# Where 16 of 256 gathered rows stand: beside the last tile's gate weights or beside the second table's first chunks

## The chip, the cores and the metric

The kernel runs on one core of one Trainium2 chip. The time is device microseconds of one execution. Timed runs are compared as medians; the profile is of one further execution, whose own time is given with it.

## The reference, cut to what matters

The program is one layer of a latent-token generator: 512 latent tokens and 256 context tokens of width 1024 go through an adaLN, two token mixers (retention and a gated linear recurrence), a merge and a residual. Then comes the part in which the change lies, a product-key expert layer. Each of the 512 tokens picks, for each of 8 heads, 16 of 16,384 single-neuron experts, so 128 experts per token, with softmax weights `g`:

```
act = gelu(einsum('thkd,td->thk', u_tab[e], xb))
out = einsum('thk,thkd->td', g * act, v_tab[e])
```

`u_tab` and `v_tab` are the first and the second table, 16,384 rows of 1024 floats each. A last residual and RMSNorm give the output.

## The kernel before, in words

The 512 tokens are four tiles of 128. Three of them (`DT = 384` tokens, `ndt = 3`) are computed densely. For each of 128 chunks of 128 experts, an S stage (`s_stage`, line 747) multiplies the chunk of the first table with the 384 tokens: load `w` (line 86), split it on ACT and DVE into high and low halves `wh` and `wl`, 24 matmuls into `pS`, and `gelu` by ACT into `gt` (line 753). At most 14 `gt` tiles are held (`RING`); the first 52 chunks (`SPILL`) are written to DRAM (`gd`) and come back later as `gr`. `pS` has two PSUM buffers, `w` two buffers, `wh` and `wl` four.

The gate weights say which expert each token uses, and with what weight. For each dense tile and each of 8 groups of 16 tokens, DVE builds one-hot tiles (lines 884 to 887: `ohB`, `ohAl`, `ohAh`, `ohAl`), TensorE multiplies them (`pw`, lines 893 and 894, 32 matmuls per group), ACT copies the products into `stg` (line 895), and SP stores `stg` to `wd` in DRAM (line 898). 24 groups make up the whole `wd`.

The second table follows in a loop of 128 chunks (line 956): load `vw`, split it into `vwh` and `vwl`, multiply `gt` or `gr` by the gate weights `wt` into `af` (line 975, DVE), split that into `ah` and `al`, and add 18 matmuls per chunk into `po`. `wt` is read back from `wd` by SP, eight chunks at a time (line 950). Each such load takes a slice of all 24 groups, so the first one waits for the last store. The S stages that are left run among these chunks.

The fourth tile (number 3, third in `TORD`) is computed by gathering. `gather_rows` (line 795) is a generator of 128 steps on the first table and 128 on the second. One step issues an indirect DMA from POOL, 128 rows of 4 KB, into one of four `row` buffers, and one DVE instruction on it (line 800, later 811). A "gathered row" below is one such step. The table of numbers in line 43, the count in line 902 and that in line 995 say how many steps have been issued by each group of the last dense tile (tile 2) and by each chunk of the second table.

The order of the instructions on each engine is fixed when the program is built: a scheduler places them by its own timeline of the program. Each engine then takes its instructions in that order, and SP and POOL issue their DMAs in that order. So a change in the number of steps can move other instructions too.

Of the kernel before, what the change touches and what calls it, by code (L numbers as in the profile page):

```python
# [39 lines left out]
NCOLS = _n  # L40
DT = 384
SPILL, RING = 52, 14
GFIRST, GSTEPS, SSTEPS = 10, 252, 124
AHEAD = 2
NROW = 4
TORD = (0, 1, 3, 2)
# [6 lines left out]
def block_kernel(ctx: ExitStack, tc: tile.TileContext, A):  # L53
# [6 lines left out]
    def split(hi, lo, src):  # L60
        S.activation(hi, src, AF.Copy)  # L61
        V.tensor_tensor(lo, src, f(hi), op=OP.subtract)  # L62

    def mm3(out, wh, wl, xh, xl, start, stop):
        PE.matmul(out, wh, xh, start=start, stop=False)  # L65
        PE.matmul(out, wh, xl, start=False, stop=False)  # L66
        PE.matmul(out, wl, xh, start=False, stop=stop)  # L67
# [693 lines left out]
    def s_more(n=1):  # L761
        nonlocal s_next
        for _ in range(n):
            if s_next < 128:
                s_stage(s_next)
                s_next += 1
# [28 lines left out]
    def gather_rows():  # L795
        for j in range(128):
            row = gp.tile([128, D], F32, name="row", bufs=4)
            G.indirect_dma_start(out=row, out_offset=None, in_=A["u"],  # L798
                                 in_offset=bass.IndirectOffsetOnAxis(ap=ei[:, j:j + 1], axis=0))
            V.scalar_tensor_tensor(row, row, 1.0, h2t, op0=OP.mult, op1=OP.mult, accum_out=act[:, j:j + 1])  # L800
            yield
        S.activation(act, act, AF.Gelu_apprx_tanh)
        V.tensor_tensor(act, act, gg, op=OP.mult)
        for j in range(128):
            row = gp.tile([128, D], F32, name="row", bufs=4)
            G.indirect_dma_start(out=row, out_offset=None, in_=A["v"],  # L806
                                 in_offset=bass.IndirectOffsetOnAxis(ap=ei[:, j:j + 1], axis=0))
            if j == 0:
                V.tensor_scalar(acc, row, act[:, j:j + 1], None, op0=OP.mult)
            else:  # L810
                V.scalar_tensor_tensor(acc, row, act[:, j:j + 1], acc, op0=OP.mult, op1=OP.add)  # L811
            yield

    with ExitStack() as es:
# [37 lines left out]
        gen = None  # L852
        for t in TORD:
            if t == ndt:
                gather_prep(p1)
                gen = gather_rows()
# [55 lines left out]
    def finish(t, src, xt):  # L912
        xo = gp.tile([128, D], F32, name="xo", tag="row", bufs=4)
        ss = gp.tile([128, 2], F32, name="ss", bufs=4)
        hs = [slice(512 * n, 512 * n + 512) for n in range(2)]
        for n, o in enumerate(hs):
            V.tensor_tensor(xo[:, o], src[:, o], g2r[:, o], op=OP.mult)
            V.tensor_tensor(xo[:, o], xo[:, o], xt[:, o], op=OP.add)
            S.activation(xt[:, o], xo[:, o], AF.Square, accum_out=ss[:, n:n + 1])
        V.tensor_tensor(ss[:, 0:1], ss[:, 0:1], ss[:, 1:2], op=OP.add)  # L920
        S.activation(ss[:, 0:1], ss[:, 0:1], AF.Sqrt, scale=1.0 / D, bias=epsc)
        V.reciprocal(ss[:, 0:1], ss[:, 0:1])
        for o in hs:
            V.scalar_tensor_tensor(xo[:, o], xo[:, o], ss[:, 0:1], fgr[:, o], op0=OP.mult, op1=OP.mult)
            SY.dma_start(A["out"][0, 128 * t:128 * t + 128, o], xo[:, o])

    def load_x1(t):
        if t in (1, 2):
            xt = ph.tile([128, D], F32, name="xt", tag="vw", bufs=2)
        else:  # L930
            xt = gp.tile([128, D], F32, name="xt", tag="row", bufs=4)
        SY.dma_start(xt, x1d[:, t])
        return xt
# [12 lines left out]
    def table(j):  # L946
        gr = j // WI
        if gr not in wts:
            wt = ph.tile([128, NG_, WI, WG], F32, name="wt" if WI * gr + WI > SPILL else "wu", bufs=2)
            SY.dma_start(wt, wd[:, :, WI * gr:WI * gr + WI, :])  # L950
            wts[gr] = wt
        return wts[gr]
# [3 lines left out]
    for n_, j in enumerate(order):  # L956
        ring = j >= SPILL
        while s_next < min(128, s_first + (128 - s_first) * (n_ + 1) // SSTEPS) or (ring and s_next <= j):
            s_more()
        if ring:  # L960
            a = Gs.pop(j)
        else:
            a = ph.tile([128, DT], F32, name="gr", bufs=2)
            SY.dma_start(a, gd[:, j])
        wt = table(j)
        v = ph.tile([128, D], F32, name="vw", bufs=2)
        vd = SY.dma_start(v, A["v"][128 * j:128 * j + 128])

        with tc.issue_after(vd.ins):
            table(order[min(n_ + 3, 127)])  # L970
        vh, vl = (ph.tile([128, D], F32R, name=f"vw{m}", bufs=2) for m in "hl")
        ah, al = (ph.tile([128, DT], F32R, name=f"a{m}", bufs=2) for m in "hl")
        split(vh, vl, v)
        af = ph.tile([128, DT], F32, name="af")
        paced = V.tensor_tensor(af.rearrange("p (g t) -> p g t", t=WG), a.rearrange("p (g t) -> p g t", t=WG), wt[:, :, j % WI], op=OP.mult)
        split(ah, al, af)
        last.append((ah, al, vh, vl))
        if n_ == 125:

            g2r, fgr = (wst.tile([128, KT, 128], F32, name=nm, tag="w").rearrange("p n m -> p (n m)") for nm in ("g2r", "fgr"))  # L980
            SY.dma_start(g2r, g2d.to_broadcast([128, D]))
            SY.dma_start(fgr, A["fg"].to_broadcast([128, D]))
            with tc.issue_after(paced.ins):
                S.activation(gp.tile([128, 1], F32, name="ws"), epsc, AF.Sqrt)
        if n_ != 126:
            for t in range(ndt):
                for n in range(2):
                    for i, (ah, al, vh, vl) in enumerate(last):
                        mm3(outs[t][:, 512 * n:512 * n + 512], ah[:, 128 * t:128 * t + 128], al[:, 128 * t:128 * t + 128],
                            vh[:, 512 * n:512 * n + 512], vl[:, 512 * n:512 * n + 512], n_ == 0, n_ == 127 and i == 1)  # L990
                if n_ == 127:
                    finish(t, outs[t], load_x1(t))
            last = []
        with tc.issue_after(paced.ins):
            while gen and done < GFIRST + GSTEPS * (n_ + 1) // 128:
                done += 1
                if next(gen, 1):
                    gen = None
                    finish(ndt, acc, load_x1(ndt))
# [64 lines left out]
```

## Time and profile before

| | us |
|---|---|
| median of 3 timed runs | 1871.71 (1871.47 to 1877.47) |
| the profiled execution's own time | 1868.65 |
| its span | 1866.9 |
| PE busy | 1812.8 (97%) |
| DVE busy | 1511.8 (81%) |
| ACT busy | 822.2 (44%) |
| POOL busy | 377.7 (20%) |

PE is TensorE, PEld its weight loads, DVE VectorE, ACT ScalarE, POOL GpSimd; SP issues most DMAs. Matmuls overlap each other, so the busy time of PE is not the time of its matmuls added up; what is told from it below is when it sat idle. Times in the trace count from the start of the span. The gate weights of tile 2 lie at about 969 to 1043 us, the second table's loop from about 1060 us to the end.

### The profile page before, as it was taken

How to read it: one execution, taken by the hardware profiler on the slowest of the kernel's cores; microseconds unless marked ns; L12 is line 12 of the kernel's file. 1: busy time of each engine (PE TensorE's matmuls, PEld its weight loads, DVE VectorE, ACT ScalarE, POOL GpSimd, SP SyncE). 2: the span in 40 equal slices, each digit the busy share in tenths (PEclk: the TensorE clock that was granted, in tenths of full speed). 3: DMA queues.
4: the chain of work that ended last, by engine and by line, in shares of the span. 5: the costliest groups of instructions: out<-in, count | busy, mean ns of one | idle time of the engine just before them, and what ended most of it. 6: DMA issues, size and time to landing. Idle time of an engine off the chain costs nothing.

```text
span 1866.9 us, 26880 instructions
## 1 busy us (share of the span) xinstructions
PE 1812.8 (97%) x9953; PEld 1598.3 (86%) x9953; DVE 1511.8 (81%) x2793; ACT 822.2 (44%) x1203; POOL 377.7 (20%) x327
## 2 busy tenths in 40 slices
PE   7899999999999999999999989999999999999997
PEld 3788888887878989999999978888888888888886
DVE  8988777788853679999988678877787878788788
ACT  4666575765222444445545433333333333333323
POOL 0000000000000000000031244444454444344440
PEclk9999999999999999999999999999999999999999
DMA  7122121215953433657778989999999899998985
GB/s 312 52 68 69 57 69 57 69 57 175 327 157 102 153 107 105 189 188 246 253 283 281 320 323 348 337 330 320 345 339 344 316 340 339 355 329 320 347 308 206
DMA packets 173320, 431.27 MB, mean 231 GB/s; under 512 B 14850, under 2 KB 84610, under 8 KB 168708
## 3 DMA queue, kind: packets, MB, share of 16 engines
q1 hardware_dynamic: 136324, 295.31, 47.0%
q0 software_dynamic: 36864, 134.23, 19.7%
q8 instruction: 78, 1.28, 0.3%
q14 instruction: 54, 0.44, 0.1%
HBM read 388.86 MB, written 40.64 MB: 230 GB/s over the span
## 4 chain that ended last, share of the span: by engine, by line
PE 75%; DVE 11%; DMA 9%; ACT 2%; issue 2%; SPq 0%; DVEq 0%; POOL 0%; ACTq 0%; POOLq 0%
PE po L65 9%; PE po L66 9%; PE po L67 9%; PE pS L65 8%; PE pS L66 8%; PE pS L67 8%; DMA vw<-in_v_dram 5%; DMA modb<-in_mod_t_dram 2%; DVE wl L62 2%; PE pw L893 1%; PE pw L894 1%; PE pu L66 1%; PE pu L67 1%; PE pu L65 1%; PE p L66 1%
## 5 line engine op out<-in xcount | busy, mean ns | idle before, releaser
L61 ACT ACTIVATE wh<-w 128x1024 fp32r<-128x1024 f32 (+1 forms) x216 | 224.9, 1043 | 340.8 <-PE pS L66 76.9
L65 PE MATMUL pS<-h2h,wh 128*128 128x384 f32 x1024 | 346.5, 338 | 2.4 <-ACT gt L753 2.2
L67 PE MATMUL pS<-h2h,wl 128*128 128x384 f32 x1024 | 345.5, 337 | 0.7 <-DVE wl L62 0.7
L66 PE MATMUL pS<-h2l,wh 128*128 128x384 f32 x1024 | 345.5, 337 | 0.0
L62 DVE TENSOR_TENSOR wl<-w,wh 128x1024 fp32r<-128x1024 f32 (+1 forms) x216 | 258.9, 1200 | 84.3 <-ACT wh L61 81.9
L798 POOL DMA_INDIRECT row<-in_u_dram,ei x128 | 190.3, 1487 | 564.3 <-DVE row L800 288.3
L66 PE MATMUL po<-vwl,ah 128*128 128x512 f32 x768 | 300.2, 391 | 0.0
L67 PE MATMUL po<-vwh,al 128*128 128x512 f32 x768 | 299.8, 391 | 0.0
L65 PE MATMUL po<-vwh,ah 128*128 128x512 f32 x768 | 267.0, 395 | 10.1 <-ACT vwh L61 10.1
L61 ACT ACTIVATE ah<-af 128x384 fp32r<-128x384 f32 x128 | 67.1, 524 | 382.1 <-PE po L66 261.1
L806 POOL DMA_INDIRECT row<-in_v_dram,ei x128 | 177.6, 1387 | 224.4 <-DVE acc L811 193.1
L65 PEld LDWEIGHTS pS<-h2h,wh 128*128 128x128 f32 x1024 | 192.6, 188 | 9.6 <-ACT gt L753 3.3
L62 DVE TENSOR_TENSOR vwl<-vw,vwh 128x1024 fp32r<-128x1024 f32 x128 | 156.3, 1221 | 53.3 <-ACT vwh L61 53.1
L67 PEld LDWEIGHTS pS<-h2h,wl 128*128 128x128 f32 x1024 | 192.5, 188 | 6.2 <-DVE wl L62 1.0
L66 PEld LDWEIGHTS pS<-h2l,wh 128*128 128x128 f32 x1024 | 192.6, 188 | 5.4
L65 PEld LDWEIGHTS po<-vwh,ah 128*128 128x128 f32 x768 | 143.0, 188 | 37.0 <-ACT vwh L61 11.7
L61 ACT ACTIVATE vwh<-vw 128x1024 fp32r<-128x1024 f32 x128 | 134.6, 1051 | 84.7 <-DMA vw<-in_v_dram 79.3
L66 PEld LDWEIGHTS po<-vwl,ah 128*128 128x128 f32 x768 | 144.3, 188 | 27.6 <-DVE vwl L62 0.4
L67 PEld LDWEIGHTS po<-vwh,al 128*128 128x128 f32 x768 | 144.4, 188 | 27.3
L811 DVE SCALAR_TENSOR_TENSOR acc<-row,act,acc 128x1024 f32<-128x1024 f32 x127 | 162.5, 1280 | 4.4 <-DMA row<-in_v_dram,ei 4.2
L800 DVE SCALAR_TENSOR_TENSOR row<-row,h2t 128x1024 f32<-128x1024 f32 x128 | 153.4, 1219 | 1.7 <-DMA row<-in_u_dram,ei 1.5
L62 DVE TENSOR_TENSOR al<-af,ah 128x384 fp32r<-128x384 f32 x128 | 71.1, 556 | 79.2 <-ACT ah L61 78.9
(368 smaller groups left out, 3489.5 us busy)
## 6 DMA issues: line engine op xcount, KB each, us to landing
w<-in_uT_dram SPq DMA_DIRECT2D x128, 512.0 KB, 4.8
vw<-in_v_dram SPq DMA_DIRECT2D x128, 512.0 KB, 6.6
w<-in_w_in_dram SPq DMA_DIRECT2D x48, 512.0 KB, 3.6
wd<-stg SPq DMA_DIRECT2D x24, 1024.0 KB, 6.0
modb<-in_mod_t_dram SPq DMA_DIRECT2D x32, 512.0 KB, 5.2
wt<-wd SPq DMA_DIRECT2D x10, 1536.0 KB, 15.9
gd<-gt SPq DMA_DIRECT2D x52, 192.0 KB, 3.3
gr<-gd SPq DMA_DIRECT2D x52, 192.0 KB, 6.7
```

Source lines behind the costliest of these rows:

```text
L61: S.activation(hi, src, AF.Copy)
L62: V.tensor_tensor(lo, src, f(hi), op=OP.subtract)
L65: PE.matmul(out, wh, xh, start=start, stop=False)
L66: PE.matmul(out, wh, xl, start=False, stop=False)
L67: PE.matmul(out, wl, xh, start=False, stop=stop)
L798: G.indirect_dma_start(out=row, out_offset=None, in_=A["u"], in_offset=bass.IndirectOffsetOnAxis(ap=ei[:, j:j + 1], axis=0))
L800: V.scalar_tensor_tensor(row, row, 1.0, h2t, op0=OP.mult, op1=OP.mult, accum_out=act[:, j:j + 1])
L806: G.indirect_dma_start(out=row, out_offset=None, in_=A["v"], in_offset=bass.IndirectOffsetOnAxis(ap=ei[:, j:j + 1], axis=0))
L811: V.scalar_tensor_tensor(acc, row, act[:, j:j + 1], acc, op0=OP.mult, op1=OP.add)
L893: PE.matmul(pw[:, i], B[:, xg, :, xi], Ah[:, xg, :, xi], start=True, stop=False)
L894: PE.matmul(pw[:, i], B[:, xg, :, xi], Al[:, xg, :, xi], start=False, stop=True)
```

## The change

Two numbers of line 43 and the expression of line 995 change:

```
-GFIRST, GSTEPS, SSTEPS = 10, 252, 124
+GFIRST, GSTEPS, SSTEPS = 26, 236, 124
...
-            while gen and done < GFIRST + GSTEPS * (n_ + 1) // 128:
+            while gen and done < GFIRST + GSTEPS * max(0, n_ - 3) // 124:
```

Before, 10 rows are issued beside the 8 groups of tile 2, and chunk `n_` brings the count to 10 + 252 (n_ + 1) // 128: 11, 13, 15 and 17 after the first four chunks, then about 1.97 more per chunk. After, 26 rows are issued beside the 8 groups (by group: 3, 6, 9, 13, 16, 19, 22, 26), none in the chunks 0 to 3, then about 1.90 per chunk. In both the generator ends in chunk 125. The S stages' own pace (`s_more`) is not edited.

On DVE, at the fifth and sixth group of tile 2, before (`row`, line 800, is a gathered row; `wl` an S stage's low half):

```order
L884 TENSOR_TENSOR ohB<-iota,e2T 128x2048
L885 TENSOR_TENSOR ohAl<-iota,e1T 128x2048
L800 SCALAR_TENSOR_TENSOR row,act<-row,h2t 128x1024
L62 TENSOR_TENSOR wl<-w,wh 128x1024
L886 TENSOR_TENSOR ohAh<-ohAl,ghT 128x2048
L884 TENSOR_TENSOR ohB<-iota,e2T 128x2048
L885 TENSOR_TENSOR ohAl<-iota,e1T 128x2048
L800 SCALAR_TENSOR_TENSOR row,act<-row,h2t 128x1024
L887 TENSOR_TENSOR ohAl<-ohAl,glT 128x2048
L62 TENSOR_TENSOR wl<-w,wh 128x1024
L886 TENSOR_TENSOR ohAh<-ohAl,ghT 128x2048
```

and the same engine at the same groups after:

```order
L884 TENSOR_TENSOR ohB<-iota,e2T 128x2048
L885 TENSOR_TENSOR ohAl<-iota,e1T 128x2048
L800 SCALAR_TENSOR_TENSOR row,act<-row,h2t 128x1024 x2
L887 TENSOR_TENSOR ohAl<-ohAl,glT 128x2048
L800 SCALAR_TENSOR_TENSOR row,act<-row,h2t 128x1024
L886 TENSOR_TENSOR ohAh<-ohAl,ghT 128x2048
L800 SCALAR_TENSOR_TENSOR row,act<-row,h2t 128x1024
L62 TENSOR_TENSOR wl<-w,wh 128x1024 x2
L887 TENSOR_TENSOR ohAl<-ohAl,glT 128x2048
L884 TENSOR_TENSOR ohB<-iota,e2T 128x2048
L885 TENSOR_TENSOR ohAl<-iota,e1T 128x2048
L800 SCALAR_TENSOR_TENSOR row,act<-row,h2t 128x1024 x3
```

The rows stand three or four to a group in place of one or two, between the one-hot instructions of a group.

On ACT, at the end of the gate weights and the start of the second table, before (`gt` is the last step of an S stage, `stg` of a gate-weight group, `ah` belongs to the first chunk of the second table):

```order
L895 ACTIVATE stg_10540<-pw_10568 128x128x4
L61 ACTIVATE wh_10850<-w_10848 128x1024
L895 ACTIVATE stg_10540<-pw_10578 128x128x4
L61 ACTIVATE wh_10957<-w_10955 128x1024
L753 ACTIVATE gt_10652<-pS_10621 128x384
L61 ACTIVATE wh_11064<-w_11062 128x1024
L753 ACTIVATE gt_10685<-pS_10654 128x384
L61 ACTIVATE wh_11169<-w_11167 128x1024
L753 ACTIVATE gt_10771<-pS_10740 128x384
L61 ACTIVATE ah_10711<-af_10715 128x384
L61 ACTIVATE vwh_10709<-vw_10707 128x1024
L753 ACTIVATE gt_10878<-pS_10847 128x384
```

and after:

```order
L895 ACTIVATE stg_10582<-pw_10610 128x128x4
L895 ACTIVATE stg_10582<-pw_10620 128x128x4
L61 ACTIVATE wh_11193<-w_11191 128x1024
L61 ACTIVATE wh_11300<-w_11298 128x1024
L61 ACTIVATE wh_11409<-w_11407 128x1024
L61 ACTIVATE ah_10759<-af_10763 128x384
L753 ACTIVATE gt_10911<-pS_10880 128x384
L61 ACTIVATE vwh_10757<-vw_10755 128x1024
L61 ACTIVATE ah_10822<-af_10826 128x384
L753 ACTIVATE gt_11009<-pS_10978 128x384
L61 ACTIVATE vwh_10820<-vw_10818 128x1024
L61 ACTIVATE ah_10854<-af_10858 128x384
```

Before, the `gt` of three S stages stand between the last `stg` and the first `ah`; after, none does, and the next `gt` stands behind that `ah`.

On SP, from the last two gate-weight stores (`wd`) to the first load of `wt`, before (`w` is an S stage's load, `vw` a chunk's of the second table):

```order
L898 DMA wd_5690<-stg_10389 128x2048
L86 DMA w_10848<-in_uT_dram 128x1024
L86 DMA w_10955<-in_uT_dram 128x1024
L898 DMA wd_5690<-stg_10540 128x2048
L86 DMA w_11062<-in_uT_dram 128x1024
L86 DMA w_11167<-in_uT_dram 128x1024
L950 DMA wt_10705<-wd_5690 128x24x128
L967 DMA vw_10707<-in_v_dram 128x1024
```

and after:

```order
L898 DMA wd_5690<-stg_10425 128x2048
L86 DMA w_11191<-in_uT_dram 128x1024
L86 DMA w_11298<-in_uT_dram 128x1024
L898 DMA wd_5690<-stg_10582 128x2048
L86 DMA w_11407<-in_uT_dram 128x1024
L86 DMA w_11511<-in_uT_dram 128x1024
L950 DMA wt_10753<-wd_5690 128x24x128
L967 DMA vw_10755<-in_v_dram 128x1024
```

The queue has the same pattern; the loads of `w` in it are those of S stages three further on.

On PE, the same 256 `pw` matmuls stand between the last transpose of tile 2's lists (line 862, `gk`) and the first `po`, with 439 `pS` matmuls before and 461 after. Of these, 323 stand ahead of the last `pw` and 116 behind it before; 440 ahead and 21 behind it after. After, the 21 belong to the S stage whose `pS` takes the PSUM buffer that `gt_10911` (in the rows of ACT above) empties.

## Rows read from the trace of the kernel before

**Rows 1.** Busy time by stretch: stretch, length, engines, PE clock, DMA share, GB/s.
```profile
969.00:1043.00 74.00, 74.00 (x592) 71.50 (x591) 63.29 (x66) 35.69 (x62) 17.57 (x10) 1.00 0.77 269
1043.00:1062.00 19.00, 19.00 (x112) 19.00 (x111) 6.92 (x8) 7.06 (x10) 0.05 (x1) 1.00 0.93 300
1062.00:1090.00 28.00, 22.07 (x101) 19.13 (x100) 18.59 (x27) 9.52 (x14) 8.89 (x7) 0.88 0.93 325
1090.00:1850.00 760.00, 755.85 (x3628) 662.00 (x3628) 621.78 (x786) 267.51 (x368) 328.83 (x235) 1.00 0.94 331
```
**Rows 2.** Waits of PE from 1043 us on: total us, times, longest.
```profile
PE po L65 <- ACT vwh L61: 10.1, 5, 5.9
```
**Rows 3.** Timeline of PE: start, us, instruction, count, idle before and releaser.
```profile
971.14 0.33 PE L65 MATMUL pS<-h2h,wh 128*128 128x384 f32 x1
...
981.37 0.34 PE L67 MATMUL pS<-h2h,wl 128*128 128x384 f32 x1
...
1042.26 0.22 PE L894 MATMUL pw<-ohAl,ohB 128*128 128x128 f16 x1
...
1062.48 0.91 PE L65 MATMUL po<-vwh,ah 128*128 128x512 f32 x3
1063.23 0.34 PE L67 MATMUL pS<-h2h,wl 128*128 128x384 f32 x1
...
1081.00 0.34 PE L66 MATMUL pS<-h2l,wh 128*128 128x384 f32 x1
1087.28 1.65 PE L65 MATMUL po<-vwh,ah 128*128 128x512 f32 x3 [5.93 <-ACT vwh L61]
1088.72 0.52 PE L67 MATMUL pS<-h2h,wl 128*128 128x384 f32 x1
...
1090.11 0.40 PE L67 MATMUL po<-vwh,al 128*128 128x512 f32 x1
```
**Rows 4.** Timeline of ACT from the last stg copies to the late vwh.
```profile
1041.35 1.57 ACT L895 ACTIVATE stg<-pw 128x512 f32<-128x512 f32 x3 [0.50 <-PE pw L894]
1043.98 1.06 ACT L61 ACTIVATE wh<-w 128x1024 fp32r<-128x1024 f32 x1 [1.05 <-DMA w<-in_uT_dram]
1044.95 0.58 ACT L895 ACTIVATE stg<-pw 128x512 f32<-128x512 f32 x1
...
1060.57 0.53 ACT L61 ACTIVATE ah<-af 128x384 fp32r<-128x384 f32 x1 [4.77 <-DVE af L975]
...
1062.29 0.47 ACT L753 ACTIVATE gt<-pS 128x384 f32<-128x384 f32 x1
...
1086.17 1.06 ACT L61 ACTIVATE vwh<-vw 128x1024 fp32r<-128x1024 f32 x1 [9.44 <-DMA vw<-in_v_dram]
```
**Rows 5.** PE by stretch, after its wait: length, busy, clock, DMA share, GB/s.
```profile
1085.00:1090.00 5.00, 2.73 (x7) 0.50 0.52 185
```
**Rows 6.** Timeline of DVE in tile 2's groups and at the first af.
```profile
969.52 2.36 DVE L885 TENSOR_TENSOR ohAl<-iota,e1T 128x2048 f16<-128x2048 f16 x2 [3.42 <-ACT e1T L868]
...
994.80 1.22 DVE L884 TENSOR_TENSOR ohB<-iota,e2T 128x2048 f16<-128x2048 f16 x1
995.94 1.22 DVE L885 TENSOR_TENSOR ohAl<-iota,e1T 128x2048 f16<-128x2048 f16 x1
...
1059.98 0.56 DVE L975 TENSOR_TENSOR af<-gt,wt 128x384 f32<-128x384 f32 x1 [3.30 <-DMA wt<-wd]
```
**Rows 7.** Timeline of SP's DMA queue up to the first load of wt.
```profile
1045.55 0.33 SPq L898 DMA_DIRECT2D wd<-stg  x1
1046.33 2.67 SPq L86 DMA_DIRECT2D w<-in_uT_dram  x2
1050.61 0.62 SPq L950 DMA_DIRECT2D wt<-wd  x1
```
**Rows 8.** From issue to landing, us: wd in 969:1043, then wt in 1043:1090.
```profile
DMA to landing us min/median/max: 5.3/7.3/7.9
...
DMA to landing us min/median/max: 9.3/14.0/18.6
```

## The prediction

> **What bounds the kernel now.** I read the table of busy times first, then the same by stretch, then PE's waits, and then the timelines of PE, ACT, DVE and SP around the one long wait. PE is busy for 97% of the span: nothing counts here but what makes PE sit idle or run slower. From 969 to 1062 us PE is busy without a break, while DVE is idle for 10.7 of the first 74 us [rows 1]. From 1043 us to the end PE waits five times for a `vwh`, 10.1 us in all, and one of these waits is 5.9 us [rows 2]. It lies from 1081.34 to 1087.28 us [rows 3]: ACT's `vwh` had waited 9.44 us for its `vw` from DRAM [rows 4], in a stretch whose DMA share is 0.93 [rows 1]. So the second table's start is late by DMA traffic, and the rest of its loop is PE's own: 755.85 of 760 us busy [rows 1].
>
> **What the change does at the start of the second table.** Seven gathered rows (17 less 10) leave the first four chunks. Each is 128 rows of 4 KB, 0.524 MB, so 3.7 MB leave; at the 325 GB/s of that stretch [rows 1] this is 11.3 us of DMA time, against a wait of 5.94 us. I take the wait as gone. With it goes a slow stretch of PE. After the wait the granted clock was 0.50, the lower of its two levels (1.2 of 2.4 GHz) [rows 5]: three `po` took 1.44 us from start to next start where they took 0.75 before it, and only from 1090.11 us on is the pace the old one [rows 3]. Of the 2.83 us from 1087.28 to 1090.11 about half is lost, 1.4 us. Together that is 7.3 us gained; the other end is nothing gained, if another transfer is late at the same place.
>
> **What it costs in the gate weights of tile 2.** 16 more DVE instructions stand there. DVE issues these at 1.14 us from start to start [rows 6]. From the first `ohAl` at 969.52 us [rows 6] to the last one of group 8 the order now holds 74 instructions of this size (32 one-hot, 26 rows, 16 `wl`), 84.4 us, so DVE is done at 1054 us if it never waits. PE reaches the products of that last group only later: the order puts 117 more `pS` ahead of the last `pw` (440, not 323). `pS` matmuls run at 0.173 us each (59 steps from 971.14 to 981.37 us [rows 3]), so 117 of them take 20.3 us, and the last `pw` starts at 1042.26 + 20.3 = 1062.5 us. DVE has some 7 us in hand by then. I cost the 16 instructions themselves at nothing: PE's own work covers them. Without that cover they are 16 x 1.14 = 18 us.
>
> **What is no longer covered.** The moved `pS` matmuls are not more work (PE does them sooner rather than later), but they were the cover for a chain. The first `af` needs `wt`; `wt` needs the last store of `wd`; that needs the last `stg`, and that the last `pw`. In the trace the chain runs: last `pw` ends at 1042.48 us [rows 3], last `stg` at 1044.95 [rows 4], its store at 1045.55, `wt` issued at 1050.61 [rows 7], `af` at 1059.98 [rows 6], `ah` from 1060.57 to 1061.10 [rows 4]. That is 18.6 us. Meanwhile PE worked on 116 `pS`, 20.2 us up to the first `po` at 1062.48 us [rows 3], so nobody saw the chain. In the new order 21 `pS` stand there, and not even these can run: they need the PSUM buffer that `gt_10911` empties, and that instruction stands on ACT's queue behind the first `ah`. So PE has nothing to do from its last `pw` until `ah` and one `gt` are done. Behind the waiting `af` on DVE stand all later `vwl` and `wl`, and behind the waiting `ah` on ACT all later `vwh`; so nothing else can feed PE either.
>
> How long is the chain then? Before, the last `stg` copy stood behind a `wh` that waited for its load: 1044.95 instead of 1042.92, where the third copy ended [rows 4]. Now the four copies follow each other, so 2.0 us less: 16.6 us. One `gt` of 0.47 us [rows 4] follows: 17.1 us of idle PE. The two `w` loads ahead of `wt` on SP wait for a `wl` each, and those `wl` for `w` loads that are issued some 6 us ahead of the last store, so I let these waits end within the 5.1 us from that store to `wt` [rows 7]. The bounds come from the landings: `wd` took 5.3 to 7.9 us, `wt` 9.3 to 18.6 [rows 8]. With the longest `wt` the idle time is 26 us. With a `wt` at the 331 GB/s of the loop [rows 1], 1.57 MB in 4.8 us, it is 12.5 us. I take 17.1, since the first `wt` of the trace stood in the same company (two `w` just ahead of it [rows 7], two `vw` behind). After it PE runs slowly again, 1.4 us by the row above.
>
> [...]
>
> **The rest of the loop.** By chunk 4 the new kernel is 8 rows ahead (27 to 19), and it gives the lead back at 0.07 rows per chunk until both end in chunk 125. So a chunk carries 3% fewer rows, and the tail is as before. The four other waits, 4.2 us in all [rows 2], may shrink or move; I leave them as they are, with 4.2 us either way.
>
> **The sum.** 1868.65 + 17.1 + 1.4 - 7.3 = 1879.9 us against the profiled execution. The median of the timed runs is 3.1 us above that execution, so I forecast 1883 us.
>
> **The rivals.**
> - The gate-weight stage itself becomes late. It would carry 16 `w` loads, 7 stores and 26 rows, 29 MB in 93.5 us, 314 GB/s, close to the loop's 331 [rows 1]. Loads of `w` that land later eat DVE's 7 us, and then `pw` and `pS` wait in PE's order. For: 269 GB/s and a share of 0.77 there now [rows 1]. Against: the slack, and that `w` stays on two buffers. Price: 4 to 10 us more, 1887 to 1893.
> - About the same time. The chain runs at its short end (12.5 us), the clock costs 1.4, the gain is 7.3 and part of the other 4.2 us goes with the rows: 1868.65 + 12.5 + 1.4 - 7.3 - 2 = 1873.3, with the offset 1876.
> - Faster. The lighter DMA traffic is what decides: all five waits of the loop go (10.1 us and 1.4 of slow clock), and the chain leaves no more than 4 us of idle PE. Then 1868.65 + 4 - 11.5 = 1861, with the offset 1864. It decides from an idle time below 10 us on. Against it: the store and the `wt` load alone took 14.4 us.
>
> **How the numbers follow.** My forecast (1877 to 1889 around 1883) has 0.60, the late gate stage 0.21, about the same 0.13, faster 0.06. A difference within 0.3% (5.6 us) can't be told from no change. So slower is 0.81, same 0.13, faster 0.06. The range that holds 8 in 10 leaves out the faster case, the lower part of the same and the far end of the late stage: 1875 to 1892 us.
>
> **What would show it.** Right: PE idle for 12 to 26 us between the last `pw` (near 1062 us) and the next `pS` or `po`, released by ACT's first `gt` behind `ah`; `af` waiting for `wt` at about 1079 us; a granted clock at half just after; no wait of several us at the third chunk. Wrong: a first `po` near 1066 us with no idle time before it, or `pw` matmuls that wait for DVE in tile 2 (then the first rival), or a 5 us wait for `vwh` in the first chunks although the rows have left.

## The result, and the profile after

The changed kernel takes 1902.29 us (median of 4 runs, 1899.85 to 1904.05), the kernel before 1872.53 us beside it (4 runs): ratio 1.0148, interval 1.0130 to 1.0167. It is slower, as forecast, but by 30 us where 11 were expected, and beyond the range's end of 1892. The profiled span is 1898.0 us against 1866.9.

The waits of PE from 960 us to the end, after (line, what ended the wait: us in all, times, longest):

```profile
PE pS L65 <- ACT gt L753: 17.7, 2, 17.4
PE po L65 <- ACT vwh L61: 10.9, 7, 3.2
PE pw L893 <- ACT stg L895: 3.9, 5, 2.4
```

Before there was one row, 10.1 us in five waits [rows 2]. Its 5.9 us wait at the third chunk is gone; three others stand in its place: one long one for `gt`, some 4 us in tile 2's gate weights, and, not foreseen, seven for `vwh` all over the loop, none longer than 3.2 us. The same by stretch (length, then busy us of PE, PEld, DVE, ACT, POOL, then granted clock, DMA share, GB/s), to be read against [rows 1]:

```profile
969.00:1043.00 74.00, 73.08 (x541) 69.99 (x540) 67.57 (x82) 30.43 (x49) 30.87 (x20) 1.00 0.85 297
```

PE no longer fills this stretch, and DVE does 4.3 us more in it than before. The timeline of PE at the end of tile 2 and the start of the second table (start, us, instruction, count, idle time before it and what ended it):

```profile
1060.15 0.22 PE L893 MATMUL pw<-ohAh,ohB 128*128 128x128 f16 x1 [2.43 <-ACT stg L895]
...
1068.61 0.22 PE L894 MATMUL pw<-ohAl,ohB 128*128 128x128 f16 x1
1086.25 0.69 PE L65 MATMUL pS<-h2h,wh 128*128 128x384 f32 x1 [17.42 <-ACT gt L753]
...
1091.85 0.48 PE L67 MATMUL pS<-h2h,wl 128*128 128x384 f32 x1
1092.17 0.34 PE L65 MATMUL pS<-h2h,wh 128*128 128x384 f32 x1
1092.35 0.33 PE L66 MATMUL pS<-h2l,wh 128*128 128x384 f32 x1
1092.70 0.86 PE L65 MATMUL po<-vwh,ah 128*128 128x512 f32 x3
```

Nothing of PE stands between 1068.83 and 1086.25 us: this is the wait that the prediction sized at 17.1. After it `pS` start 0.32 us apart instead of 0.175, up to 1092.17 us, in all 5.9 us at half pace. The clock says the same (stretch, length, busy us, granted clock, DMA share, GB/s; 0.50 is the level of 1.2 GHz, 1.00 that of 2.4):

```profile
1085.00:1090.00 5.00, 3.75 (x12) 3.75 (x13) 4.17 (x7) 3.59 (x6) 0.00 (x0) 0.50 0.61 217
1090.00:1095.00 5.00, 5.00 (x22) 4.59 (x21) 0.60 (x1) 0.00 (x0) 0.00 (x0) 0.78 1.02 304
...
1165.00:1170.00 5.00, 3.98 (x13) 3.54 (x14) 3.97 (x6) 3.76 (x5) 0.30 (x1) 0.72 0.77 295
```

The last row lies in the loop: after a wait of PE of 1.84 us there, up to 1166.02 us, the clock falls as well. Why the gap is as long as it is shows on SP, ACT and DVE. First SP's queue:

```profile
1038.00 8.44 SPq L898 DMA_DIRECT2D wd<-stg  x2
1046.55 1.83 SPq L86 DMA_DIRECT2D w<-in_uT_dram  x2
...
1069.80 0.33 SPq L898 DMA_DIRECT2D wd<-stg  x1
1071.99 1.46 SPq L86 DMA_DIRECT2D w<-in_uT_dram  x2
1073.89 0.63 SPq L950 DMA_DIRECT2D wt<-wd  x1
```

Then ACT:

```profile
1055.99 1.06 ACT L61 ACTIVATE wh<-w 128x1024 fp32r<-128x1024 f32 x1 [4.05 <-DMA w<-in_uT_dram]
1058.56 1.06 ACT L61 ACTIVATE wh<-w 128x1024 fp32r<-128x1024 f32 x1 [1.51 <-DMA w<-in_uT_dram]
1059.52 2.04 ACT L895 ACTIVATE stg<-pw 128x512 f32<-128x512 f32 x4
1067.70 2.06 ACT L895 ACTIVATE stg<-pw 128x512 f32<-128x512 f32 x4 [6.15 <-issue]
...
1085.30 0.52 ACT L61 ACTIVATE ah<-af 128x384 fp32r<-128x384 f32 x1 [8.17 <-DVE af L975]
1085.72 0.47 ACT L753 ACTIVATE gt<-pS 128x384 f32<-128x384 f32 x1
```

And DVE:

```profile
1040.61 1.22 DVE L800 SCALAR_TENSOR_TENSOR row<-row,h2t 128x1024 f32<-128x1024 f32 x1
...
1044.04 1.22 DVE L886 TENSOR_TENSOR ohAh<-ohAl,ghT 128x2048 f16<-128x2048 f16 x1
1045.18 2.35 DVE L62 TENSOR_TENSOR wl<-w,wh 128x1024 fp32r<-128x1024 f32 x2
...
1084.70 0.56 DVE L975 TENSOR_TENSOR af<-gt,wt 128x384 f32<-128x384 f32 x1 [6.32 <-DMA wt<-wd]
```

The chain, link by link: last `pw` ends 1068.83, last `stg` 1069.76, store issued 1069.80, `wt` issued 1073.89, `af` 1084.70, `ah` 1085.30, `gt` ends 1086.19. And ahead of it, in tile 2: the two `w` loads of 1046.55 us come late. On SP the second of the two `wd` stores in the row above them waits for its `stg` copies and is issued only at 1046.12 us. Without that store they could not have gone much sooner either: their two buffers are freed by the two `wl` of 1045.18 us, which end at 1046.40 and 1047.53, and ahead of those stand three gathered rows and an `ohAh` on DVE. Then the loads land late as well, the first after 9.4 us (in the kernel before, from 969 to 1060 us, the median of such loads is 5.4). Beside them run the gathers of six rows. The share of the DMA engines' time that POOL's queue took from 1044 to 1060 us (packets, MB, share), first in the kernel before, then in the changed one:

```profile
q0 software_dynamic: 4, 0.01, 0.2%
```

```profile
q0 software_dynamic: 842, 3.08, 56.7%
```

The second `w` let ACT start its `wh` only at 1058.56 us, some 11 us after its issue, and four `stg` copies, with the `pw` that need the buffers they empty, stood behind it.

To see all stretches at once, I added up two things over stretches of 5 us: the idle time of PE, and its busy time times (1 less the granted clock), which is what the slow clock costs. "Gate" is 960 to 1060 us, "start" 1060 to 1100, "loop" 1100 to 1840. The rows of the experiments below stand here too.

| kernel | span | gate: idle, clock | start: idle, clock | loop: idle, clock | sum |
|---|---|---|---|---|---|
| before | 1866.9 | 0, 0 | 5.9, 1.6 | 4.1, 0 | 11.6 |
| after | 1898.0 | 3.2, 0 | 18.4, 4.4 | 10.9, 4.4 | 41.3 |
| e1 26 rows, no pause | 1894.2 | 1.6, 0.7 | 16.3, 3.0 | 13.1, 4.8 | 39.5 |
| e2 pause alone | 1861.7 | 0.5, 0 | 0.2, 0 | 6.0, 1.6 | 8.3 |
| e3 26 rows, 96 `pS` held back | 1896.9 | 20.7, 3.9 | 2.0, 1.7 | 11.2, 5.4 | 44.9 |
| e4 18 rows | 1892.5 | 1.0, 0 | 13.2, 2.8 | 15.1, 8.5 | 40.6 |
| e5 14 rows | 1878.4 | 0, 0 | 9.4, 2.7 | 8.2, 3.2 | 23.5 |
| e6 6 rows | 1872.6 | 2.4, 0.2 | 0, 1.4 | 9.1, 3.1 | 16.2 |
| e7 before, 11 rows | 1888.9 | 3.1, 1.6 | 4.6, 1.5 | 16.4, 6.6 | 33.8 |
| e8 after, `wt` read twice only | 1878.0 | 2.9, 0 | 17.6, 3.7 | 0.7, 0 | 24.9 |
| e9 after, `wt` in quarters | 1875.8 | 3.8, 0.3 | 16.4, 2.8 | 0.8, 0 | 24.1 |
| e10 pause, `wt` in quarters | 1855.2 | 0.7, 0 | 0, 0 | 0.4, 0 | 1.1 |
| e11 before, `wt` in quarters | 1854.6 | 0, 0 | 1.1, 0 | 0.4, 0 | 1.5 |

After less before is 29.7 of the 31.1 us in the spans: 3.2 in the gate weights, 15.3 at the start, 11.2 in the loop. Each row is one execution, and executions of one kernel differ: the 18 timed runs of the kernel before beside e1 to e4 lie between 1858.76 and 1881.31 us, and e4, e6 and e7 were profiled in runs that were 4.8, 6.6 and 3.7 us above their medians. So the rows for the loop rank kernels only roughly.

### The profile page after: what moved, and what is told of

Its sections match the earlier page's. It is cut to its first block, busy times and chain, and to the rows that moved or that the text cites. A ratio compares the mean times of both kernels' runs of the same rounds, so it can differ in the third digit from the quotient of the medians.

```text
span 1898.0 us, 26889 instructions
## 1 busy us (share of the span) xinstructions
PE 1821.3 (96%) x9953; PEld 1604.0 (85%) x9953; DVE 1514.0 (80%) x2793; ACT 821.5 (43%) x1203; POOL 393.6 (21%) x327
## 5 line engine op out<-in xcount | busy, mean ns | idle before, releaser
L61 ACT ACTIVATE wh<-w 128x1024 fp32r<-128x1024 f32 (+1 forms) x216 | 224.7, 1043 | 340.9 <-DMA w<-in_uT_dram 87.0
L798 POOL DMA_INDIRECT row<-in_u_dram,ei x128 | 202.8, 1584 | 565.2 <-DVE row L800 284.3
L65 PE MATMUL po<-vwh,ah 128*128 128x512 f32 x768 | 267.0, 395 | 10.9 <-ACT vwh L61 10.9
L61 ACT ACTIVATE vwh<-vw 128x1024 fp32r<-128x1024 f32 x128 | 134.4, 1050 | 110.5 <-DMA vw<-in_v_dram 101.9
```

The lines of the kernel that those rows point to most:

```text
L798: G.indirect_dma_start(out=row, out_offset=None, in_=A["u"], in_offset=bass.IndirectOffsetOnAxis(ap=ei[:, j:j + 1], axis=0))
```

## The experiments

All timed ratios are against the kernel before, run beside them (1871.63 us for e1 to e4, 1869.54 for e5 to e8, 1871.03 for e9 to e11).

**e1 and e2: the two parts of the change apart.** e1 has the changed numbers and the old expression, e2 the old numbers and the pause.

```
e1: GFIRST, GSTEPS = 26, 236    GFIRST + GSTEPS * (n_ + 1) // 128
e2: GFIRST, GSTEPS = 10, 252    GFIRST + GSTEPS * max(0, n_ - 3) // 124
```

> The change's first part alone: 26 rows beside the last dense tile's gate weights, and rows again from chunk 0 on (26 + 236 (n_ + 1) // 128). The order on PE is that of the changed kernel around the last pw: 21 pS behind it. Theory A (cover: the lost time is the chain from the last pw to the first ah, which the order leaves without work on PE): 16 to 19 us of idle PE before the first po, released by gt, and 1895 to 1905 us. Theory B (traffic: the moved rows' transfers make the loads late, and the lull in the first four chunks is made up for by denser rows later): with the rows spread again the late waits for vwh in the loop fall back to 4 us or less and the time to 1885 to 1892.

> The change's second part alone: 10 rows beside the gate weights as before, none in the first four chunks, then 252 (n_ - 3) // 124, 2.03 per chunk. The order on PE keeps 116 pS behind the last pw. Theory A: no idle time before the first po, the 5.9 us wait for vwh at the third chunk and its slow clock go (7.3 us), 1864 to 1869 us. Theory B: the wait goes, but denser rows bring it back later in the loop (waits for vwh of 8 us or more after 1100 us, as in the changed kernel), 1871 to 1878.

e1: 1900.14 us, ratio 1.0170 (1.0137 to 1.0203), with the long wait (16.3 us) and the loop's waits. e2: 1866.29 us, ratio 0.9985 (0.9961 to 1.0009), no wait over 1 us at the start. So the loss is that of the 26 rows alone. The pause takes away the wait at the third chunk, 5.9 us in the profile, but as a time it can't be told from no change.

**e3: the cover put back, with 26 rows.** The last four S stages ahead of the loop are issued behind the last `pw`, so that 96 `pS` stand there in place of 21.

```
-                    s_more((SPILL + RING - 1) * slots // NG_ - s_next)
+                    s_more(min((SPILL + RING - 1) * slots // NG_, SPILL + RING - 1 - HOLD) - s_next)
...
+        with tc.issue_after(lastpw.ins):
+            s_more(SPILL + RING - 1 - s_next)
```

> The changed kernel with the last four S stages that come ahead of the second table queued on PE behind the last pw (96 pS behind it, not 21). The rows stay where the change puts them. Theory A: the 17.4 us of idle PE before the first po fall below 5 us; in exchange PE waits for DVE inside the gate weights (its own work there shrinks by some 29 us, DVE's doesn't), about 5 to 10 us in sum; 1885 to 1894 us. Theory B: the traffic is the same, so 1898 to 1906.

1899.31 us, ratio 1.0170 (1.0137 to 1.0203): nothing won. The idle time at the start is down to 2.0 us, and stands in tile 2 instead (waits of PE, 960 us to the end; line numbers are up to one higher here):

```profile
PE pw L895 <- DVE ohAl L888: 13.1, 4, 5.1
PE po L66 <- ACT vwh L62: 12.1, 6, 2.9
PE pw L894 <- ACT stg L896: 4.5, 4, 2.3
PE pw L894 <- DVE ohAh L887: 3.0, 2, 1.6
```

Without those `pS` PE reaches the products before DVE has built their one-hot tiles. The `pS` that used to cover the chain now cover DVE; they can't do both. My expectation that the cover would bring the time back failed here.

**e4, e5, e6: how many rows.** 18, 14 and 6 rows beside tile 2, with the pause; 50, 80 and 105 `pS` stand behind the last `pw` (before 116, after 21).

```
e4: GFIRST, GSTEPS = 18, 244
e5: GFIRST, GSTEPS = 14, 248
e6: GFIRST, GSTEPS = 6, 256
```

> 18 rows beside the gate weights in place of 26, none in the first four chunks, then 244 (n_ - 3) // 124. 50 pS stand behind the last pw, where 21 (26 rows) and 116 (10 rows) do. Theory A: idle time before the first po between the two, 8 to 14 us, and 1880 to 1892 us. Theory B: half of the traffic moved, half of the loss: 1885 to 1889, with the idle time before the first po near 17 us.

> 14 rows beside the gate weights, none in the first four chunks, then 248 (n_ - 3) // 124. 80 pS stand behind the last pw (13.9 us of cover for a chain of some 17 us). Theory A (cover): 3 to 6 us idle before the first po. For the loop's larger waits two theories. O (order): they grow with the number of chunks whose first po stands right behind the last po of the chunk before, with no pS between: 37 of the first 120 before, 63 in the changed kernel, 69 here, so 10 us or more of waits for vwh after 1100 us and 1878 to 1886 us. S (the late start itself, or the 26 rows, leaves the loop badly placed): with a nearly undisturbed start the loop loses 4 to 7 us, as in the kernel with the pause alone, 1868 to 1874 us.

> 6 rows beside the gate weights, none in the first four chunks, then 256 (n_ - 3) // 124, 2.06 per chunk: the change's direction reversed in its first part. 105 pS stand behind the last pw, and DVE has 4 instructions fewer ahead of it. Theory A (cover): no idle time before the first po, no long wait at the third chunk; 1860 to 1868 us. O (45 chunks without pS ahead): waits for vwh after 1100 us of 5 to 8 us. B (traffic: rows that leave the gate weights make the loop's loads later): 10 us or more of such waits, 1872 to 1880.

Idle time at the wait for `gt`: 14.2 us with 50 `pS`, 9.4 with 80, none with 105 (a `po` waits 2.4 there). Times: 1889.48 (1.0083, 1.0048 to 1.0118), 1880.86 (1.0056, 1.0033 to 1.0079) and 1867.78 (1.0000, 0.9976 to 1.0023). The wait falls with the cover, as the theory of the chain has it, if only those `pS` are counted that can run: none of the 21 in the changed kernel, 29 of the 50 in e4 and 56 of the 80 in e5 start before the wait; the others need what stands behind the first `ah`. From after to e4 the 29 cover 5.1 us, but the chain from the last `pw` to the end of the first `ah` is 1.9 us longer (18.9, not 17.0): 17.4 - 5.1 + 1.9 = 14.2. From e4 to e5 27 more cover 4.7 us of the same chain (18.8): 9.5. My 3 to 6 us for e5 had counted all 80. The loop's waits (15.1, 8.2 and 9.1 us idle) do not fall in step with the number of rows. Nor do they follow a count that I had tried, of chunks with no `pS` ahead of their first `po`: 60 in e4, 69 in e5, 45 in e6.

**e7: one row moved.** The kernel before with 11 rows in place of 10, and no pause.

```
-GFIRST, GSTEPS, SSTEPS = 10, 252, 124
+GFIRST, GSTEPS, SSTEPS = 11, 251, 124
```

> The kernel before with 11 rows in place of 10 beside the gate weights and 11 + 251 (n_ + 1) // 128 after: one row is moved, next to no traffic, but the order comes out otherwise: 102 pS behind the last pw, and 53 of 120 chunks without pS ahead of their first po (37 before). A: no idle time before the first po, and the 5.9 us wait at the third chunk stays. O: waits for vwh after 1100 us of 7 to 12 us and 1874 to 1880 us. S: 4 us of such waits, and the time of before, 1870 to 1873.

1887.06 us, ratio 1.0087 (1.0059 to 1.0114). The DMA traffic of the loop is one row of 246 lighter, and the loop alone loses 18.9 us more than before. Its 16.4 us of idle time are more than any of my theories gave (7 to 12 at most):

```profile
PE po L65 <- ACT vwh L61: 19.5, 9, 4.5
```

So how long the loop's waits are is no matter of how many bytes the rows bring. What is left as the cause is the order, which the scheduler makes anew for each set of numbers.

**e8: without the reloads of `wt`.** The changed kernel, reading only two groups of `wt`, one for the spilled chunks and one for the others; 14 of the 16 loads are left out (the expectation below says 13 of 15), and the later chunks use the gate weights of the first.

```
-        gr = j // WI
+        gr = SPILL // WI if j // WI >= SPILL // WI else 0
```

> The changed kernel, leaving out every load of the gate weights wt after the first one of each of its two kinds (13 of 15 loads of 1.5 MB; the later chunks use the first tables again, so the gate weights of later chunks are not the right ones). All theories: the 17 us before the first po stay. If vw comes late in the loop because it lands behind a wt load, the 10.9 us of waits for vwh after 1100 us fall below 2 us and with them the slow clock behind them, 1885 to 1890 us; if the order alone makes them (69 chunks without pS ahead here), they stay near 10 us and the time near 1900.

One run, 1879.75 us, below the 1885 to 1890 that I had written; of the loop's 10.9 us of waits 0.7 are left, and no slow clock. The gap at the start stays (16.3 us). The waits need the `wt` loads. How, SP's queue shows, in the changed kernel (`wu` is the `wt` of the spilled chunks):

```profile
1259.72 0.54 SPq L950 DMA_DIRECT2D wt<-wd  x1
1260.48 7.07 SPq L86 DMA_DIRECT2D w<-in_uT_dram  x1
1267.66 0.53 SPq L967 DMA_DIRECT2D vw<-in_v_dram  x1
1268.24 0.77 SPq L950 DMA_DIRECT2D wu<-wd  x1
1269.11 16.18 SPq L86 DMA_DIRECT2D w<-in_uT_dram  x1
```

Two loads of 1.57 MB follow each other closely, and the issue of the next load takes 16.18 us in place of 0.33. The `vw` issued between the two loads lands late; ACT's `vwh` waits 7.55 us for it, and PE for that:

```profile
1281.25 1.06 ACT L61 ACTIVATE vwh<-vw 128x1024 fp32r<-128x1024 f32 x1 [7.55 <-DMA vw<-in_v_dram]
```

```profile
1282.35 0.97 PE L65 MATMUL po<-vwh,ah 128*128 128x512 f32 x3 [2.14 <-ACT vwh L61]
```

The kernel before has such a place near here too, with an issue of 12.32 us at 1248.93 and a wait of PE of only 0.43 us at 1269.01. In both kernels the issue just behind each of the 16 loads holds the queue for over 2 us, 111 us in all before and 117 after. So what differs must be what stands behind the loads in the order, not that they are there; this is argued from the two traces, no run shows it by itself.

**e9, e10, e11: the same bytes in quarters.** Each `wt` load is cut into four of 0.39 MB by groups of 16 tokens, pieces of 512 B as before, one behind the `vw` of each of four chunks, 6 to 3 chunks ahead. e9 is the changed kernel so, e10 the pause alone, e11 the kernel before.

```
-            table(order[min(n_ + 3, 127)])
+            for p in range(1, WP + 1):
+                table(order[min(n_ + 3 + WP - p, 127)], p)
...
+        while p < parts:
+            g0, g1 = NG_ * p // WP, NG_ * (p + 1) // WP
+            SY.dma_start(wt[:, g0:g1], wd[:, g0:g1, WI * gr:WI * gr + WI, :])
+            p += 1
```

> The changed kernel with each load of eight chunks' gate weights (1.57 MB, 13 of the 15 of them in the loop's course) cut into four of 0.39 MB, one issued behind the vw of each of four successive chunks, 6, 5, 4 and 3 chunks ahead, in place of one whole load 3 chunks ahead. Bytes and piece sizes as before; 21 pS behind the last pw, as in the changed kernel. Theory Q (the loop's waits come from vw loads that stand on SP behind a whole 1.57 MB load): a vw stands behind a quarter of it at most, so the waits of the loop's po for vwh fall from 10.9 to 1-4 us and the slow clock from 4.4 to under 2; the idle time at the start, 17 us, stays; span 1884 to 1891. Theory T (the waits come from the number of bytes in flight, wherever they stand in the queue): loop as it was, 8 to 12 us of waits, span 1895 to 1900.

> The kernel before with only the pause in the first four chunks, and the gate-weight loads cut into four as in e9; 116 pS behind the last pw, as in the kernel before. Theory Q: the loop's idle time falls from 6.9 (with 1.6 of slow clock) to 1-3 us, nothing at the start, span 1854 to 1859 against 1861.7 for the pause alone, ratio to the kernel before 0.991 to 0.996. Theory T: as the pause alone, 1861 to 1864, ratio 0.998.

> The kernel before, no row moved, with the gate-weight loads cut into four as in e9. The first two loads still come whole. Theory Q: the other loop waits (4.1 us) fall to 0-2; the 5.9 us wait at the third chunk, in which vw stands behind the first whole load, stays at 4-7: span 1861 to 1865, ratio 0.996 to 0.999. Theory T: nothing moves, 1866 to 1868, ratio 1.0. If the order that the scheduler makes of the new kernel brings its own waits, it shows in this run alone as over 6 us of loop waits.

| | us (6 runs each) | ratio | span |
|---|---|---|---|
| e9 | 1879.70 | 1.0056 (1.0034 to 1.0077) | 1875.8 |
| e10 | 1853.33 | 0.9912 (0.9891 to 0.9933) | 1855.2 |
| e11 | 1856.96 | 0.9929 (0.9907 to 0.9950) | 1854.6 |

Theory Q holds and T falls: in all three the loop's idle time is 0.4 to 0.8 us. e9's span is even 8 us under what Q gave; the sums in the table account for 17.2 of the 22.2 us by which it is shorter than the changed kernel's. The pieces are also issued up to three chunks earlier than the whole load was, and no run separates that from their size. PE's waits in e9, 960 us to the end, and SP's queue where two such loads meet as they did above:

```profile
PE pS L65 <- ACT gt L753: 16.4, 1, 16.4
PE pw L893 <- ACT stg L895: 3.8, 5, 2.4
PE po L66 <- DVE vwl L62: 0.8, 1, 0.8
```

```profile
1249.30 0.69 SPq L973 DMA_DIRECT2D vw<-in_v_dram  x1
1250.03 0.77 SPq L955 DMA_DIRECT2D wu<-wd  x1
1251.14 2.60 SPq L955 DMA_DIRECT2D wt<-wd  x1
1253.86 3.51 SPq L86 DMA_DIRECT2D w<-in_uT_dram  x1
1257.47 1.22 SPq L973 DMA_DIRECT2D vw<-in_v_dram  x1
```

No issue near there takes over 3.51 us, and ACT's `vwh` of 1100 to 1840 us wait 18.0 us in all for their `vw`, not 101.9:

```profile
  DMA vw<-in_v_dram: 101.9, 30
```

```profile
  DMA vw<-in_v_dram: 18.0, 10
```

The first of these is the changed kernel, the second e9. In e11 the waits of PE are down to one row:

```profile
PE po L66 <- DVE vwl L62: 1.5, 2, 1.1
```

Here my expectation missed: the 5.9 us wait at the third chunk, which I had left standing, went too, and the kernel won 0.7% where 0.1 to 0.4% was written. The second load does not come whole here, as I had thought: two of its pieces stand behind the first `vw` (1054.11 us) and one behind each of the next two. In the kernel before that `vw` was issued just behind the second whole `wt` load, and the issue itself took long:

```profile
1065.44 0.61 SPq L950 DMA_DIRECT2D wt<-wd  x1
1067.34 8.36 SPq L967 DMA_DIRECT2D vw<-in_v_dram  x1
```

So the wait that the change was weighed against goes without moving a row. e10 beats both kernels; it is not told from e11 (six runs each, 1852.22 to 1856.94 and 1853.92 to 1859.02 us).

With the loads in quarters the change can also be priced without the loop's waits: e9 over e11 is 1879.70 - 1856.96 = 22.7 us, and their sums in the table differ by 22.6 (16.4 and 2.8 at the start, less e11's 1.1; 4.1 in the gate weights; 0.4 more in the loop).

## Why the prediction was right and wrong

**Right: what is no longer covered.** The wait lies between the last `pw` and the first `pS`, ended by the `gt` behind `ah`, as written: 17.42 us against 17.1. Link by link: last `pw` to the store 1.0 us, store to `wt` 4.1 (5.1 in the trace of before), `wt` to `af` 10.8 (9.4 before), `af` to `pS` 1.6. That the sum comes so close is in part luck: the store took 1.0 us less and the load 1.4 more than in the trace of before. e4, e5 and e6 show the mechanism by giving the cover back in steps.

**Right, with half of the cause: the third chunk.** The wait of 5.94 us is gone. I had put it down to the rows' DMA time, and e2 bears that out: taking the rows away ends it, though the second `wt` load still stands whole ahead of that `vw` on SP. The load lands after 10.5 us in place of 18.6, and the issue of `vw` takes 5.03 us in place of 8.36:

```profile
1061.83 0.53 SPq L950 DMA_DIRECT2D wt<-wd  x1
1063.19 5.03 SPq L967 DMA_DIRECT2D vw<-in_v_dram  x1
```

But e11 ends the wait with all rows in place. So, as far as two runs with new orders can show it, the wait took both, the rows' traffic and a whole `wt` load ahead of the `vw`; the second half was not in my working.

**Wrong, the step that failed most: "the rest of the loop".** I left the loop's other waits at 4.2 us, give or take 4.2, since they come from chunks with 3% fewer rows. Measured are 10.9 us idle and 4.4 of slow clock, 11.2 more than before. The working took these waits as a matter of traffic. What the runs show in its place is that they come from loads that stand on SP behind a whole `wt` load (10.9 us idle with whole loads, 0.8 with the same bytes in quarters, e9), and that an edit of the numbers changes how long they are with next to no change of traffic (e7, one row: 16.4 us, 4.1 before). In the kernels with whole loads and an edited number they are 6.0 to 16.4 us (e1 to e7). No rival named it.

**Wrong in size: the slow clock.** I carried over 1.4 us from the kernel before, where PE had been idle for 5.9 us and ran at half pace for 2.8 [rows 3, 5]. After 17.4 us of idle time it ran at half pace for 5.9, a loss of 3.0; another 1.4 followed the waits of the last `pw`.

**Wrong in part: the gate weights "at nothing".** In the changed kernel no `pw` waits for a one-hot tile, but DVE's slack was mostly gone: it was done at 1062.01 us, not at 1054, and e3 shows how near that is (16.1 us of waits for `ohAl` and `ohAh` as soon as the `pS` go). And the last `pw` came at 1068.6, not 1062.5 us. The first rival had the place, the price (4 to 10 us; measured 5.6 with the slow clock) and the cause: loads of `w` that land late, beside the rows' gathers. What it had not seen is the way that the delay took: not through DVE's one-hot tiles, but through ACT's queue, where the `wh` that waited for its load stood ahead of `stg`, and so to `pw`. The rows on DVE had a share in it, since they stand ahead of the `wl` that free the buffers of `w`. This is read from the one trace; no run moved those rows or loads by themselves.

The sum with the measured terms: 1868.65 + 17.4 + 3.0 - 7.5 (the wait and the slow clock at the start, before) = 1881.6 for what the prediction spoke of; 11.2 in the loop and 5.6 in the gate weights (3.2, 1.0 after 1060 us, and 1.4 of clock) make 1898.4, of the 1899.85 us that the profiled execution took.

**What stays open.** Which feature of an order sets how long the loop's waits are with whole loads: neither the rows, nor the cover, nor the count of chunks without `pS` ranks e1 to e7, as far as one profile of each can rank them. Whether the quarters help by their size, by being issued earlier or by being spread was not separated. An order with the rows moved and the loop's order kept as it was before was not tried. Nor was the chain shortened (a smaller first `wt` load), so whether 26 rows could be carried at no cost is not known.

## What to carry to other kernels

Work that is moved away may have been the cover of a chain: list what the engine did between the chain's first and last link, and count how much of it is left and can run without the chain. Before a wait for a DMA is put down to traffic, look at the issuing queue: here an issue of 8 or 16 us in place of 0.3 meant that a large load stood just ahead, and cutting that load into pieces among the urgent ones cost no bytes and took the waits away. Where a scheduler orders the program, a change of one in a table of numbers is a new order: what it does to waits far from the edit belongs in the range.

## What the runs showed of the hardware

- In the kernel before and in the changed one, the issue on SP just behind each of the 16 loads of 1.57 MB held the queue for 2.1 to 16.2 us (8.36, 12.32 and 16.18 are named above); no other issue from 1045 us on took over 2 us, and the median is 0.33. With the loads in quarters the longest was 4.7 us in e9, 5.3 in e10 and 7.6 in e11. The Trainium skill (DMA: Bandwidth & Descriptors, section on queues, rings and completion order) says that each DMA engine consumes a ring's descriptors in order; that agrees with `vw` landing late behind `wt` (ACT waited 7.55 us for the one of 1267.66 us).
- The Trainium skill (DMA: Bandwidth & Descriptors, section on rules for kernel authors) asks for 1 MiB or more per DMA for bandwidth. Here pieces of 0.39 MB cost none: 333 GB/s over the loop in e11 (1100 to 1840 us), 334 before, and e11 was faster by 0.7%.
- After an idle time PE ran at half pace for 2.8 us (before, 5.9 us idle), 6.1 (e6, 4.6 idle at 1425 us), 5.5 (e5, 9.4 idle), 3.5 (e9, 16.4 idle) and 5.9 (after, 17.4 idle). The length of the idle time does not order them, so a loss carried over from one wait to a longer one, as the prediction did, can be off either way.
- 16 more gathered rows beside the one-hot tiles did not slow DVE's instructions: its 1.22 us for a one-hot tile is the same before [rows 6] and after (the `ohAh` of 1044.04 us).
